# Loading two token groups of a hybrid layer in both layouts, instead of transposing them on TensorE

## The chip, the cores and the metric

The kernel runs on one core of one Trainium2 chip. Its time is the device time of one execution in microseconds (us). A core has a matrix engine (TensorE, PE in the profile, with PEld for its weight loads), a vector engine (VectorE, DVE), a scalar engine (ScalarE, ACT), GpSimd (POOL) and SyncE (SP), whose queue issues most of the DMA transfers here. Each engine works through its own list of instructions in order and waits on semaphores for the others. On-chip data lies in SBUF, and matmul results land in PSUM; 128 partitions each.

## The reference

One layer of a hybrid network over 1280 tokens: 256 context tokens (`ctx`) and 1024 latent tokens (`x`), 1024 features each. Cut to what matters for the change, its first step is

```
h   = rms_norm(tokens, g)                     # per token: x * rsqrt(mean(x*x) + 1e-6) * g
h   = h * (1 + scale) + shift                 # per feature; scale, shift from c (latents) or c_ctx (context)
u   = h @ w_in                                # one combined input projection, 1024 features in
...                                           # short convs, gated delta rule, retention, gates,
...                                           # output projection, residual, SwiGLU, residual, final norm
```

The factor of the norm belongs to a token; gain, scale and shift belong to a feature. All of it is float32 in the reference.

## The kernel before

**Stages.** The program runs in five parts, by the trace: the stage "h" (modulated tokens, first columns of the projection; to about 111 us), the rest of the projection with short convolutions (to about 300), chunks of the gated delta rule and retention (to about 580), and then the output projection and the SwiGLU part up to 1476 us.

**The stage "h".** Matmuls contract over the partition axis, so the tokens are needed with features on partitions: `hhi` and `hlo` hold the modulated tokens as eight tiles (index `k`, 128 features each) by 1280 tokens. A float32 value is split in two: `hhi` is the value rounded to the short format `fp32r`, `hlo` what is left. The product with a weight `whi + wlo` is then three matmuls (`tm_half`, L366 to L373: `whi·hhi` on L371, `wlo·hhi` on L372, `whi·hlo` on L373), 24 of them for a token tile of 128 tokens and a group `g` of output columns (272 columns for g=0, 256 for g=1).

**Token groups.** Tiles of 128 tokens are handled in four groups, `XGROUPS = [[2, 3], [4, 5], [6, 7, 8, 9], [0, 1]]` (tiles 0 and 1 are the context). In the text they are called group 0 to 3. For each group:

- `normalize` (L319): ACT squares each token tile and sums it (L325), DVE takes the reciprocal root (`rsqrt_mean`, last instruction L139), and DVE multiplies each loaded tile, tokens on partitions, by its factors in place (L328).
- `turned` (L330): PE transposes 128x128 blocks through a matmul with `ident` into a PSUM bank `xtr` (L334); one bank holds one `k` of all the group's tokens.
- `modulate` (L307): ACT writes `hhi` from that bank with scale and shift as per-partition operands (L311), DVE computes the same value in full float32 as `hf` (L313, two buffers), and `hlo = hf - hhi` is computed by DVE for even `k` and by GpSimd for odd `k` (L314).
- PE runs the 24 matmuls for each tile, first all tiles of the group for g=0, then for g=1; three PSUM banks `tm` take the results, ACT copies them out (L384 and L402), and they are stored.

The modulated tokens of group 2 are made while PE works on group 1, those of group 3 while PE works on group 2.

**What sets the order.** The program text goes through a scheduler that simulates the engines and fixes each engine's list. An edit can therefore move rows that it doesn't touch. The loads of this stage are chained one behind the other on SyncE's queue by `in_order` (L235); the token tiles have seven buffers.

**Behind the stage.** `ada_rest` loads more modulation weights (`adaw2`, L495), accumulates them on DVE (L497, L499, into `acc`) and sums over partitions on PE (L504, into `gr`). The convolution part of the projection starts with L611. Its buffers take the room of the stage's own, so its loads on SyncE's queue wait until that is free.

Of the kernel before, what the change touches and what calls it, by code (L numbers as in the profile page):

```python
# [8 lines left out]
F32 = mybir.dt.float32  # L9
# [8 lines left out]
P = 128  # L18
# [20 lines left out]
def build(nc, tc, ap, dbg=None, stop=None, marks=None):  # L39
# [19 lines left out]
    def close(p):  # L59
        p_close.pop(id(p)).close()  # L60
# [130 lines left out]
    try:  # L191
# [115 lines left out]
        def modulate(src, k, j, sl):  # L307

            n = sl.stop - sl.start
            a, b = amix[:, j, k:k + 1], bmix[:, j, k:k + 1]  # L310
            hh = S.activation(hhi[:, k, sl], src, AF.Identity, bias=b, scale=a)  # L311
            hf = P0.tile([P, 512], F32, tag="hf", name="hf", bufs=2)
            V.tensor_scalar(hf[:, :n], src, a, b, ALU.mult, ALU.add)  # L313
            (G if k % 2 else V).tensor_tensor(hlo[:, k, sl], hf[:, :n], hhi[:, k, sl].bitcast(F32), ALU.subtract)  # L314
            return hh.ins

        XGROUPS = [[2, 3], [4, 5], [6, 7, 8, 9], [0, 1]]

        def normalize(gi, hold=None):  # L319
            grp = XGROUPS[gi]  # L320
            ms = P0.tile([P, len(grp)], F32, tag="ms%d" % gi, name="ms")
            with tc.issue_after(hold) if hold is not None else nullcontext():
                for i, t in enumerate(grp):
                    junk = P0.tile([P, D], F32, tag="junk", name="junk", bufs=1)
                    S.activation(junk, xts[t], AF.Square, accum_out=ms[:, i:i + 1])  # L325
                rstd = rsqrt_mean(P0, ms, len(grp), "rx%d" % gi, D)
            for i, t in enumerate(grp):
                V.tensor_scalar(xts[t], xts[t], rstd[:, i:i + 1], None, ALU.mult)  # L328

# [7 lines left out]
        def modulated(gi):  # L337
            grp = XGROUPS[gi]
            for k in range(KT):
                end = modulate(turned(gi, k, bank_b), k, 1 if grp[0] == 0 else 0, slice(grp[0] * P, (grp[-1] + 1) * P))  # L340
            return end

        def split(raw, hi, lo, e):
# [100 lines left out]
            begin(3)  # L444
        ada_end = coefficients(1)
        close(PA)
        W2 = pool("w2", bufs=2)
        xa = W2.tile([P, TT, 16], F32, tag="xa", name="xa", bufs=1)
        raw_weights(1, 0, W2)
# [3 lines left out]
        for n in ("alog", "dtb"):  # L453
            small[n] = C.tile([P, 8], F32, tag=n, name=n)
            in_order(small[n], ap[n].partition_broadcast(P))
        for t in (6, 7, 8, 9, 0, 1):
            load_x(t)
        hold = None
        for k in range(4, KT):
            hold = modulate(xnT[:, k, :], k, 0, slice(2 * P, 4 * P))  # L460
        normalize(1, hold)
        for gi, grp in enumerate(XGROUPS):
            for g in range(2):
                if gi == 0 and g == 1:
                    for kh in range(2):
                        wr[1, kh] = tm_weights(1, kh, W2)
                for t in grp:
                    if (g, t) in first:
                        o = first[g, t]
                    else:  # L470
                        o = tm_bank(g)
                        tm_half(o, wr[g, 0], 0, t)
                    tm_half(o, wr[g, 1], 1, t)
                    tm_store(g, t, o, fin_copy, S, W2)
                if g == 0 and gi + 1 < len(XGROUPS):
                    hold = modulated(gi + 1)
            if gi + 2 < len(XGROUPS):
                normalize(gi + 2, hold)
        close(P0)
        checkpoint("h")  # L480

# [1129 lines left out]
def prepare(inputs):  # L1611
# [2 lines left out]
    a = {}  # L1614
    a["x"] = f(inputs["x"])[0]
    a["ctx"] = f(inputs["ctx"])[0]
    a["cc"] = f(np.stack([np.asarray(inputs["c"])[0], np.asarray(inputs["c_ctx"])], -1).reshape(KT, P, 2).transpose(1, 0, 2))
    ada_w = np.asarray(inputs["ada_w"])[0]
    a["ada1"] = f(ada_w[:, :2 * D].reshape(KT, P, 2, 2, 512).transpose(3, 0, 1, 2, 4))
# [35 lines left out]
```

## Time and profile before

| what | value |
|---|---|
| median of 3 runs | 1481.49 us (1479.01 to 1481.59) |
| profiled execution | 1477.96 us, span 1476.2 us |
| mean granted TensorE clock | 0.983 |
| PE busy | 1397.2 us, 95% |
| DVE busy | 964.6 us, 65% |
| ACT busy | 614.0 us |
| POOL busy | 590.3 us |

A row of a timeline gives the start in us, the duration in us, the engine, the source line, the operation, output and inputs by their names in the program, the tile's shape, and after "x" how many of them follow each other; in square brackets stands how long the engine had been idle before, and what released it. A row of windows gives a stretch of time, and for each engine the time busy in it with the number of instructions. Source lines (L...) are lines of the kernel before unless said otherwise.

### The profile page before, as it was taken

The numbers are of one execution on the slowest core, as the hardware profiler recorded it, in microseconds if no ns is written. First come the engines' busy times: TensorE is split into PE (matmuls) and PEld (weight loads), VectorE is DVE, ScalarE is ACT, GpSimd is POOL, SyncE is SP. The second block draws the span as 40 slices with busy tenths as digits, with TensorE's granted clock in tenths as the row PEclk, the third lists the DMA queues.
The fourth block names the chain that finished last, engine by engine and source line by source line (L and its number), as shares of the span: only waits on it lengthen the run. The fifth ranks groups of instructions, "written<-read, shape, count | busy, mean of one in ns | idle before, by whom it ended". The sixth has DMA issues, their size and how long they took to land.

```text
span 1476.2 us, 24111 instructions
## 1 busy us (share of the span) xinstructions
PE 1397.2 (95%) x8919; PEld 1199.2 (81%) x8919; DVE 964.6 (65%) x1856; ACT 614.0 (42%) x1326; POOL 590.3 (40%) x501
## 2 busy tenths in 40 slices
PE   7999999986789999899799899999999999999997
PEld 2898888975689999898688688877888888788885
DVE  6566789289792435689676877556555564657477
ACT  5643564587333111245443623233333332444445
POOL 0120010243202344234144688898555552335321
PEclk9999999998899999999899999999999999999999
DMA  9536686688888625996532265674222242776863
GB/s 337 197 105 205 189 249 200 219 264 277 282 216 277 238 76 178 416 341 209 184 125 104 97 238 210 242 264 162 105 97 105 107 151 79 260 260 194 288 216 114
DMA packets 170421, 298.14 MB, mean 202 GB/s; under 512 B 43496, under 2 KB 93880, under 8 KB 165952
## 3 DMA queue, kind: packets, MB, share of 16 engines
q1 hardware_dynamic: 118752, 253.17, 50.2%
q10 hardware_dynamic: 49072, 35.83, 7.8%
q0 software_dynamic: 2480, 7.60, 1.4%
q8 instruction: 70, 1.15, 0.3%
q14 instruction: 47, 0.39, 0.1%
HBM read 206.60 MB, written 89.96 MB: 201 GB/s over the span
## 4 chain that ended last, share of the span: by engine, by line
PE 55%; POOL 6%; DMA 5%; DVE 4%; issue 2%; ACT 2%; SPq 1%; ACTq 0%; POOLq 0%; DVEq 0%
PE ffn L1344 7%; PE ffn L1342 6%; PE ffn L1343 6%; PE fo L1470 4%; PE fo L1469 4%; PE fo L1468 4%; PE tm L371 3%; PE tm L373 3%; PE tm L372 3%; PE op L1203 2%; PE op L1201 2%; PE op L1202 2%; DMA wd<-tw 2%; POOL ws L1315 1%; DMA pk<-sd 1%
## 5 line engine op out<-in xcount | busy, mean ns | idle before, releaser
L371 PE MATMUL tm<-whi,hhi 128*128 128x256 f32 (+1 forms) x704 | 199.5, 287 | 7.7 <-ACT vt L859 3.4
L372 PE MATMUL tm<-wlo,hhi 128*128 128x256 f32 (+1 forms) x704 | 199.3, 285 | 2.4 <-issue 2.0
L373 PE MATMUL tm<-whi,hlo 128*128 128x256 f32 (+1 forms) x704 | 197.7, 285 | 0.0
L371 PEld LDWEIGHTS tm<-whi,hhi 128*128 128x128 f32 x704 | 132.8, 190 | 11.8 <-ACT vt L859 3.6
L1342 PE MATMUL ffn<-t,whi 128*128 128x512 f32 x352 | 136.9, 390 | 1.3 <-ACT whi L344 1.3
L1344 PE MATMUL ffn<-t,wlo 128*128 128x512 f32 x352 | 137.0, 390 | 1.0 <-DVE wlo L345 1.0
L1343 PE MATMUL ffn<-t,whi 128*128 128x512 f32 x352 | 137.0, 389 | 0.0
L372 PEld LDWEIGHTS tm<-wlo,hhi 128*128 128x128 f32 x704 | 133.7, 190 | 2.1 <-issue 0.9
L373 PEld LDWEIGHTS tm<-whi,hlo 128*128 128x128 f32 x704 | 132.8, 190 | 2.6 <-issue 1.8
L344 ACT ACTIVATE whi<-wraw 128x512 fp32r<-128x512 f32 (+2 forms) x98 | 75.1, 771 | 141.4 <-PE ffn L1343 80.5
L344 ACT ACTIVATE whi<-ws 128x512 fp32r<-128x512 f32 x88 | 55.6, 632 | 171.5 <-PE ffn L1343 123.4
L345 DVE TENSOR_TENSOR wlo<-ws,whi 128x512 fp32r<-128x512 f32 x88 | 93.9, 1068 | 47.0 <-ACT whi L344 46.8
L1469 PE MATMUL fo<-wlo,ahi 128*128 128x512 f32 x308 | 120.2, 390 | 2.1 <-DVE wlo L345 2.1
L1468 PE MATMUL fo<-whi,ahi 128*128 128x512 f32 x308 | 119.3, 390 | 0.7 <-ACT ahi L344 0.7
L1470 PE MATMUL fo<-whi,alo 128*128 128x512 f32 x308 | 119.0, 390 | 0.0
L345 DVE TENSOR_TENSOR wlo<-wraw,whi 128x512 fp32r<-128x512 f32 (+2 forms) x92 | 99.4, 1082 | 24.6 <-ACT whi L344 24.6
L1342 PE MATMUL ffn<-b,whi 128*128 128x512 f32 x264 | 103.8, 393 | 4.4 <-ACT whi L344 4.4
L1344 PE MATMUL ffn<-b,wlo 128*128 128x512 f32 x264 | 103.6, 393 | 0.8 <-DVE wlo L345 0.8
L1343 PE MATMUL ffn<-b,whi 128*128 128x512 f32 x264 | 103.4, 392 | 0.0
L612 PE MATMUL b<-hlo,whi 128*128 128x512 f32 (+1 forms) x256 | 94.4, 369 | 0.0
L613 PE MATMUL b<-hhi,wlo 128*128 128x512 f32 (+1 forms) x256 | 94.3, 368 | 0.0
L611 PE MATMUL b<-hhi,whi 128*128 128x512 f32 (+1 forms) x256 | 94.3, 368 | 0.0
(446 smaller groups left out, 3448.1 us busy)
## 6 DMA issues: line engine op xcount, KB each, us to landing
adaw<-ada SPq DMA_DIRECT2D x48, 512.0 KB, 4.4
pk<-sd SPq DMA_DIRECT2D x16, 1536.0 KB, 10.0
wraw<-wfi SPq DMA_DIRECT2D x44, 512.0 KB, 3.7
ar<-ad SPq DMA_DIRECT2D x33, 512.0 KB, 4.7
w<-wfo SPq DMA_DIRECT2D x22, 512.0 KB, 5.7
wd<-tw SPq DMA_DIRECT2D x11, 1024.0 KB, 4.8
ad<-act SPq DMA_DIRECT2D x20, 512.0 KB, 3.0
raw<-wd SPq DMA_DIRECT2D x20, 512.0 KB, 4.9
```

Of the source, the lines that this page charges most:

```text
L344: S.activation(hi, raw, AF.Copy)
L345: e.tensor_tensor(lo, raw, hi.bitcast(F32), ALU.subtract)
L371: T.matmul(o, hhi[:, k, tsl], whi[:, k % 4, :], start=(k == 0), stop=False)
L372: T.matmul(o, hhi[:, k, tsl], wlo[:, k % 4, :], start=False, stop=False)
L373: T.matmul(o, hlo[:, k, tsl], whi[:, k % 4, :], start=False, stop=(k == KT - 1))
L612: T.matmul(o, whi[:, k, :], hl, start=False, stop=False)
L1342: T.matmul(o, whi[:, k, :], xhi(xn, slice(0, 4), k), start=(first and k == 0), stop=False, **kw)
L1343: T.matmul(o, whi[:, k, :], xlo(xn, slice(0, 4), k), start=False, stop=False, **kw)
L1344: T.matmul(o, wlo[:, k, :], xhi(xn, slice(0, 4), k), start=False, stop=(k == 3), **kw)
L1468: T.matmul(po[g][i], ahi[:, ts], whi, start=(j == 0 and not kw), stop=False, **kw)
L1469: T.matmul(po[g][i], ahi[:, ts], wlo, start=False, stop=False, **kw)
L1470: T.matmul(po[g][i], alo[:, ts], whi, start=False, stop=(j == FH - 1), **kw)
```

## The change

For groups 2 and 3 the tokens are also loaded with features on partitions, from a second copy of the tokens in device memory that is stored that way (`xT`): eight tiles of 128x512 for group 2 and eight of 128x256 for group 3, in eight buffers of one size. The tiles with tokens on partitions are still loaded, since the sums of squares are taken from them. The in-place scaling of these tiles (L328) and the transposes (L334) of the two groups are gone. In their place the factors of a group are turned into a row that is the same on all partitions: for each token tile `ident` is multiplied by the factors (DVE, tile `diag`, two buffers), a matmul of `ones` with that diagonal puts the factors on every partition (PE, bank `rrow`), DVE copies the bank to SBUF, and each `xT` tile is multiplied by it in place (DVE). `modulate` then reads `xT` in SBUF instead of a PSUM bank. Lines of the changed kernel below the first added block stand 9 lines further down, then 18, 23, 24, 28 and, behind the stage, 29.

```
+        def load_xT(gi):
+            grp = XGROUPS[gi]
+            for k in range(KT):
+                xt = PX[0].tile([P, 512], F32, tag="xT", name="xT", bufs=8)
+                xTs[gi, k] = xt[:, :len(grp) * P]
+                in_order(xTs[gi, k], ap["xT"][k, :, grp[0] * P:(grp[-1] + 1) * P])
...
         def normalize(gi, hold=None):
...
+            if gi >= 2:
+                pr = bank_b("rrow")
+                for i in range(len(grp)):
+                    dg = PX[0].tile([P, P], F32, tag="diag", name="diag", bufs=2)
+                    V.tensor_scalar(dg, ident, rstd[:, i:i + 1], None, ALU.mult)
+                    T.matmul(pr[:, i * P:(i + 1) * P], ones, dg, start=True, stop=True)
+                rrow[gi] = PX[0].tile([P, 512], F32, tag="rrow", name="rrow", bufs=1)
+                V.tensor_copy(rrow[gi][:, :len(grp) * P], pr[:, :len(grp) * P])
+                return
             for i, t in enumerate(grp):
                 V.tensor_scalar(xts[t], xts[t], rstd[:, i:i + 1], None, ALU.mult)
...
         def modulated(gi):
             grp = XGROUPS[gi]
             for k in range(KT):
-                end = modulate(turned(gi, k, bank_b), k, 1 if grp[0] == 0 else 0, slice(grp[0] * P, (grp[-1] + 1) * P))
+                if gi >= 2:
+                    src = xTs[gi, k]
+                    V.tensor_tensor(src, src, rrow[gi][:, :len(grp) * P], ALU.mult)
+                else:
+                    src = turned(gi, k, bank_b)
+                end = modulate(src, k, 1 if grp[0] == 0 else 0, slice(grp[0] * P, (grp[-1] + 1) * P))
...
         close(PA)
+        PX.append(pool("px", side="right"))
...
-        for t in (6, 7, 8, 9, 0, 1):
+        for t in (6, 7, 8, 9):
             load_x(t)
+        load_xT(2)
+        for t in (0, 1):
+            load_x(t)
+        load_xT(3)
...
+        close(PX[0])
         close(P0)
...
+    a["xT"] = f(np.concatenate([a["ctx"], a["x"]], 0).T.reshape(KT, P, NTOK))
```

On the vector engine the work for group 2 changes its order. Names here: `rx2y` are the factors of group 2's tokens, `rrow` is the row of factors (bank and copy). Before, from the scaling of group 2's tiles on:

```order
L328 TENSOR_SCALAR xt<-xt,rx2y 128x1024 x4
L313 TENSOR_SCALAR hf<-xtr,amix,bmix 128x512 x2
L314 TENSOR_TENSOR hlo<-hf,hhi 128x512
L313 TENSOR_SCALAR hf<-xtr,amix,bmix 128x512 x2
```

and in the changed kernel at the same place:

```order
L340 TENSOR_SCALAR diag<-ident,rx2y 128x128 x4
L343 COPY rrow<-rrow 128x512
L360 TENSOR_TENSOR xT<-xT,rrow 128x512 x8
L313 TENSOR_SCALAR hf<-xT,amix,bmix 128x512 x2
L314 TENSOR_TENSOR hlo<-hf,hhi 128x512
```

All eight multiplications stand ahead of the first `hf` and the first `hlo`, where before the first `hf` followed the scaling directly.

On TensorE, the end of group 1's work and the start of group 2's (the first rows with 272 columns), before:

```order
L373 MATMUL tm<-whi,hlo 128x256
L334 MATMUL xtr<-ident,xt 128x128 x12
L371 MATMUL tm<-whi,hhi 128x272
L372 MATMUL tm<-wlo,hhi 128x272
L371 MATMUL tm<-whi,hhi 128x272
L372 MATMUL tm<-wlo,hhi 128x272
L371 MATMUL tm<-whi,hhi 128x272
L372 MATMUL tm<-wlo,hhi 128x272
L334 MATMUL xtr<-ident,xt 128x128 x8
L373 MATMUL tm<-whi,hlo 128x272
```

and in the changed kernel (its L394, L395 and L396 are L371, L372 and L373 of before):

```order
L396 MATMUL tm<-whi,hlo 128x256
L341 MATMUL rrow<-diag,ones 128x128 x4
L394 MATMUL tm<-whi,hhi 128x272
L395 MATMUL tm<-wlo,hhi 128x272
L394 MATMUL tm<-whi,hhi 128x272
L395 MATMUL tm<-wlo,hhi 128x272
L394 MATMUL tm<-whi,hhi 128x272
L395 MATMUL tm<-wlo,hhi 128x272
L396 MATMUL tm<-whi,hlo 128x272
```

The transposes are gone and four matmuls with `ones` stand where the first twelve were; the first matmul with `hlo` still stands behind three pairs with `hhi`, as before.

On SyncE's queue the eight loads of group 2's `xT` come between the last latent tiles and the first context tile, and those of group 3 behind the second context tile:

```order
L238 DMA xt<-x 128x1024 x4
L238 DMA xT<-xT 128x512 x8
L238 DMA xt<-ctx 128x1024
L377 DMA wraw<-wt 128x1024 x2
L238 DMA xt<-ctx 128x1024
L238 DMA xT<-xT 128x256 x8
L524 DMA adaw_1240<-ada 128x1024
```

Before, the same rows stood there without the two of `xT`; the first of the `adaw` loads (L495 before, L524 now) comes behind them.

More of the change, by code (lines that the diff above doesn't have):

```diff
@@ L315, in modulate @@
             return hh.ins
+        xTs, rrow, PX = {}, {}, []
+        def load_xT(gi):
[4 more added lines that the diff above has]
+                in_order(xTs[gi, k], ap["xT"][k, :, grp[0] * P:(grp[-1] + 1) * P])
         XGROUPS = [[2, 3], [4, 5], [6, 7, 8, 9], [0, 1]]
```

## The prediction

> **What bounds the kernel now.** I read first how busy the engines are in each stretch of the program, cut where TensorE changes its work: end of group 1, group 2 with g=0, group 2 with g=1, group 3, the convolution part, the chunks. Columns: each engine's busy time with instructions, the granted TensorE clock, the DMA share and GB/s.
>
> ```profile
> core 0: us, PE busy (x) PEld busy (x) DVE busy (x) ACT busy (x) POOL busy (x), PEclk, DMA share, GB/s
> 60.00:68.37 8.37, 7.08 (x58) 6.87 (x57) 2.87 (x10) 6.04 (x15) 0.74 (x1) 1.00 0.35 110
> 68.37:83.35 14.98, 13.82 (x107) 12.52 (x105) 11.45 (x20) 9.26 (x17) 5.90 (x4) 1.00 0.13 45
> 83.35:99.63 16.28, 16.28 (x137) 16.28 (x137) 7.64 (x17) 7.85 (x19) 3.16 (x4) 1.00 0.31 100
> 99.63:111.37 11.74, 11.74 (x98) 11.74 (x97) 9.14 (x14) 4.19 (x10) 2.39 (x1) 1.00 0.64 207
> 100.00:300.00 200.00, 200.00 (x1229) 175.52 (x1228) 142.79 (x244) 99.70 (x275) 23.33 (x20) 1.00 0.68 215
> 300.00:480.00 180.00, 147.48 (x2005) 135.41 (x2004) 134.68 (x275) 92.81 (x233) 45.81 (x48) 0.94 0.87 262
> ```
>
> TensorE is busy all the time from 83 to 300 us, so there what delays it delays the end, and work taken off it in group 2's second half and in group 3 is time saved. The one place where the changed work meets something else is 68.37 to 83.35: TensorE lacks 1.16 of 14.98 us, and VectorE is at 11.45 us, the next bound. So I read that stretch row by row, first on TensorE.
>
> ```profile
> 68.37 1.94 PE L334 MATMUL xtr<-ident,xt 128*128 128x128 f32 x12
> 70.97 0.39 PE L371 MATMUL tm<-whi,hhi 128*128 128x272 f32 x1 [0.65 <-ACT hhi L311]
> 71.82 1.39 PE L334 MATMUL xtr<-ident,xt 128*128 128x128 f32 x8
> 73.16 0.39 PE L373 MATMUL tm<-whi,hlo 128*128 128x272 f32 x1
> 75.53 1.03 PE L334 MATMUL xtr<-ident,xt 128*128 128x128 f32 x8
> 78.64 0.60 PE L334 MATMUL xtr<-ident,xt 128*128 128x128 f32 x4
> 83.35 0.39 PE L371 MATMUL tm<-whi,hhi 128*128 128x272 f32 x1 [0.30 <-ACT xa L384]
> 99.63 0.29 PE L371 MATMUL tm<-whi,hhi 128*128 128x272 f32 x1
> 111.37 0.28 PE L611 MATMUL b<-hhi,whi 128*128 128x256 f32 x1
> ```
>
> The 32 transposes of group 2 come in four lots among the matmuls of its first three tiles; the fourth tile starts at 83.35. Then VectorE, GpSimd and ScalarE in the same place:
>
> ```profile
> 66.77 0.16 DVE L139 SCALAR_TENSOR_TENSOR rx2y<-rx2u,rx2y 128x4 f32<-128x4 f32 x1
> 66.97 2.74 DVE L328 TENSOR_SCALAR xt<-xt,rx2y 128x1024 f32<-128x1024 f32 x4
> 70.95 1.56 DVE L313 TENSOR_SCALAR hf<-xtr,amix,bmix 128x512 f32<-128x512 f32 x2 [1.24 <-ACT hhi L311]
> 72.42 0.68 DVE L314 TENSOR_TENSOR hlo<-hf,hhi 128x512 fp32r<-128x512 f32 x1
> 78.85 1.17 DVE L314 TENSOR_TENSOR hlo<-hf,hhi 128x512 fp32r<-128x512 f32 x1
> 72.58 1.66 POOL L314 TENSOR_TENSOR hlo<-hf,hhi 128x512 fp32r<-128x512 f32 x1 [10.72 <-DVE hf L313]
> 78.17 1.29 POOL L314 TENSOR_TENSOR hlo<-hf,hhi 128x512 fp32r<-128x512 f32 x1 [1.35 <-DVE hf L313]
> 70.13 2.12 ACT L311 ACTIVATE hhi<-xtr,bmix,amix 128x512 fp32r<-128x512 f32 x3 [1.18 <-PE xtr L334]
> ```
>
> The factors are there at 66.93, and the first `hlo` at 73.10; the first matmul that reads it (L373) starts at 73.16. That handover sets the pace, and it is what I follow through the change.
>
> **The change part by part. The row of factors.** Four diagonals of 128x128 on VectorE stand for 2.74 us of scaling. No row has this shape; the nearest are
>
> ```profile
> 29.54 0.73 DVE L313 TENSOR_SCALAR hf<-xnT,amix,bmix 128x256 f32<-128x256 f32 x2
> 31.84 1.02 DVE L313 TENSOR_SCALAR hf<-xnT,amix,bmix 128x256 f32<-128x256 f32 x2
> 30.75 1.64 POOL L314 TENSOR_TENSOR hlo<-hf,hhi 128x256 fp32r<-128x256 f32 x1 [30.31 <-ACT hhi L311]
> 99.37 0.48 DVE L497 TENSOR_SCALAR acc<-adaw,csl 128x512 f32<-128x512 f32 x1
> 276.29 1.95 PE L705 MATMUL kk<-kc 128*128 128x128 f32 x16
> L932 DVE COPY S<-up x2: 691/692/692, 485.2 to 486.1; 128x512 f32<-128x512 f32 x2
> 830.13 1.88 DVE L345 TENSOR_TENSOR wlo<-wraw,whi 128x512 fp32r<-128x512 f32 x3
> ```
>
> Half of 0.73 is 0.37 at 256 columns, so 0.2 to 0.37 at 128; I take 0.3. Diagonals 0 and 1 are done by 67.6, and TensorE is free from group 1 at 68.37. A float32 matmul of 128x128 shows as two passes, 1.95/16 = 0.12 each, so 0.24. With two `diag` buffers, diagonals 2 and 3 wait for the first two matmuls; the four matmuls end near 69.95. The copy from PSUM costs 0.69 (the only row of that size): the row stands at 70.65, where before the scaled tiles stood at 69.71.
>
> **The multiplications.** Eight of 128x512 with both inputs in SBUF. L345's row gives one such as 0.68 (also the lone `hlo`) and then 1.88 - 0.68 = 1.20 for two, 0.60 each. The eight take 0.68 + 7·0.60 = 4.9 us, to 75.5, and by the order on VectorE all stand ahead of the first `hf`. Then two `hf`, now from SBUF instead of PSUM: 0.48 and 0.44 (L497's row, 0.48, against 1.56/2 = 0.78 before), to 76.45, and `hlo` 0.68, to 77.1. ScalarE is no limit: the first `hhi` can start when the first multiplication ends, 71.3, and ends 2.12/3 = 0.7 later, 72.0; TensorE's first L371 moves from 70.97 to 72.1, does three pairs, and waits for the first `hlo`: from 73 to 77.1. Before, transposes filled part of that time; they are gone, so the gap is bare.
>
> **What this makes of group 2.** From 77.1, 66 of the 72 matmuls of three tiles remain, at 11.74/98 = 0.12 (last stage in the windows): 7.9 us, to 85.0, and with the wait of 0.30 before it the fourth tile starts at 85.3 instead of 83.35: +2.0. That holds if the later `hlo` keep up. They keep up only if GpSimd's and VectorE's shares run side by side. The rows say that they don't: the `hlo` at 78.85 took 1.17, and ended at 80.02, which is 79.46 (GpSimd's end) + 0.56, where the lone one took 0.68; the pair of `hf` from SBUF at 31.84 took 1.02 instead of 0.73 with GpSimd running until 32.39. Before, `hf` read PSUM and shows no such wait; now all of VectorE's work there reads SBUF. With strict turns (GpSimd 1.1 of its own) the `hlo` of k = 0 to 7 come at 77.1, 78.3, 79.4, 81.6, 82.2, 84.7, 85.4 and 87.35, the fourth tile starts at 88.1: +4.7. The Trainium skill (SBUF — State Buffer, "Who interferes with whom") states that a VectorE instruction with two SBUF inputs or in a two-port mode and a GpSimd instruction that reads SBUF exclude each other for a whole instruction; by that rule the upper of the two sums holds, and the trace's 1.17 against 0.68 agrees.
>
> **Group 3.** Its 16 transposes lie in the full stretch from 83.35 to 99.63:
>
> ```profile
> 86.83 0.49 PE L334 MATMUL xtr<-ident,xt 128*128 128x128 f32 x3
> 91.17 0.38 PE L334 MATMUL xtr<-ident,xt 128*128 128x128 f32 x2
> ```
>
> Three take 0.49 with a last drain of 0.29, so 0.10 each at the least, and 0.15 by the lot at 68.37 ((1.94-0.29)/11): 1.6 to 2.4 us, I take 1.7. Its two matmuls for the row cost 2·0.24 = 0.5, so -1.2. VectorE has the room for the rest: 7.64 of 16.28 us are busy, and two scalings go while eight multiplications of half the size come (about 8·0.35 = 2.8 us). The stage as a whole: +0.8 without exclusion, +3.5 with; nearest to the rows is the second, and I take **+3.0**.
>
> **Behind the stage.** The sums that the convolution part starts with:
>
> ```profile
> 111.30 0.65 DVE L499 SCALAR_TENSOR_TENSOR acc<-adaw,csl,acc 128x512 f32<-128x512 f32 x1
> 113.13 1.02 PE L504 MATMUL gr<-acc,ones 128*1 128x512 f32 x2
> ```
>
> `acc` is done at 111.95, 0.58 after TensorE's stage ends at 111.37. The matmul on it (L504) stood some 15 matmuls behind the first L611; in the new order it stands ahead of it. If the chain moves with the stage, TensorE waits about 0.6 us: **+0.5**, between 0 (the chain is not moved) and +1.5. The added 3 MB of loads fall on a DMA share of 0.13 to 0.35, and the weights behind them are first used after 104 us: 0, and what would uncover them is the second rival. The order also differs between 280 and 480 us, where TensorE lacks 180 - 147.48 = 32.5 us; I know no sign for that: 0, between -3 and +3.
>
> **Sum:** 3.0 + 0.5 = +3.5. The profiled execution took 1477.96 us, 3.5 below the median; I add the difference to the median: 1481.49 + 3.5 = **1485.0**.
>
> **The rivals.** (a) No change that can be measured (0.2% is about 3 us): the engines overlap after all, +0.8 in the stage, and the later order gives or takes two: 1479.5 to 1484, middle 1482. For it: GpSimd's idle of 1.35 between its `hlo` shows slack. Against it: the gap before the first L373 does not depend on the overlap. (b) SyncE's queue.
>
> ```profile
> 70.87 14.67 SPq L495 DMA_DIRECT2D adaw<-ada  x2
> 59.71 0.33 SPq L238 DMA_DIRECT2D xt<-ctx  x1
> ```
>
> The eight loads of group 3's `xT` each wait for a buffer of group 2, freed as late as 87 by the last `hf`, and the `adaw` loads (before: waited until 85.2) stand behind them. If the first of these then lands 3 us later than the stage moves, the whole chain to L504 does, and TensorE stands at L504: +3 more, 1488. Against it: these loads waited for the stage's memory anyway, and the last four are paced by `acc`. (c) The other side: the saving comes through. If the scheduler's list doesn't hold `hlo` back (the first by 73 us, as when the multiplications run between the `hf`), 5.1 us of transposes of group 2 (1.94 + 1.39 + 1.03 + 0.60 = 4.96 by the rows, with the pauses at their ends) and 1.2 us of group 3 are gone, less 1 us for the later row of factors: about -5, 1476. The point from which it decides is a first `hlo` before about 74 us. Against it: the list has all eight multiplications first.
>
> **How the numbers follow.** My forecast gets 0.45, with a range of its own from +1 to +7: 0.30 of it slower by over 0.2%, 0.15 within. Rival (a) 0.25: 0.22 within, 0.03 faster. Rival (b) 0.15, slower. Rival (c) 0.15: 0.10 faster, 0.05 within, where part of the saving is eaten. Together: faster 0.13, same 0.42, slower 0.45. The range: 1478.5 leaves out most of (c), 1491 some of (b) and the top of the later order's luck, together about 0.18. The likeliest case alone runs from 1482.5 to 1488.5.
>
> **What the profile will show.** Right if eight multiplications of about 0.6 us stand on VectorE from about 70.7 to 75.5; if TensorE then idles about 4 us before its first matmul with `hlo`, released by VectorE; if `hlo` rows on either engine stretch past their lone durations; if the fourth tile of group 2 starts 2 to 5 us later than 83.35, the convolution part 1 to 4 later than 111.37, and 111 to 300 keeps its length within 1 us. Wrong if the first `hlo` comes by 74 us, if the multiplications take 0.4 us or less, or if most of the difference arises after 280 us, where I set it to 0.

## The result

| | median | runs | ratio to before |
|---|---|---|---|
| before | 1479.24 us | 9, 1477.88 to 1481.59 | |
| changed | 1486.66 us | 9, 1481.74 to 1488.86 | 1.0041, 95% interval 1.0028 to 1.0054 |

The change makes the kernel slower by 0.41%, 6.1 us (0.0041 · 1479.24). The two medians lie 7.4 us apart, which is inside the interval of the ratio (4.1 to 8.0 us); the sums below go by the 6.1. The forecast was +3.5 us and slower, with a range from 1478.5 to 1491. The profiled execution of the changed kernel took 1486.66 us (span 1484.8, granted clock 0.974 against 0.983).

### The profile after

First the place where all was expected to happen, the start of group 2. Windows of the changed kernel, with the columns of the table shown for the kernel before:

```profile
69.00:73.92 4.92, 2.41 (x20) 2.03 (x18) 3.00 (x8) 1.25 (x3) 0.00 (x0) 0.92 0.14 46
73.92:78.80 4.88, 1.72 (x6) 1.40 (x6) 4.84 (x10) 4.88 (x8) 0.51 (x1) 0.50 0.01 3
78.80:83.28 4.48, 4.48 (x20) 4.48 (x21) 4.38 (x6) 2.50 (x6) 2.56 (x2) 0.50 0.45 127
83.28:90.00 6.72, 6.46 (x47) 5.88 (x47) 6.08 (x17) 0.84 (x4) 2.94 (x2) 0.99 0.25 73
```

TensorE (first busy time) works 4.1 of 9.8 us between 69 and 78.8. VectorE (third) works 3.00 of 4.92 us in the first window, where it waits for TensorE's row of factors (1.30 and 0.58 us), and 4.84 of 4.88 us in the second. The granted clock is at half (0.50) from 73.2 to 83.4. Before, TensorE worked 13.82 of the 14.98 us from 68.37 to 83.35, and the clock was 1.00. TensorE's rows of the changed kernel:

```profile
70.85 0.71 PE L341 MATMUL rrow<-diag,ones 128*128 128x128 f32 x4 [0.16 <-DVE diag L340]
73.92 0.59 PE L394 MATMUL tm<-whi,hhi 128*128 128x272 f32 x1 [2.35 <-ACT hhi L311]
75.22 0.43 PE L395 MATMUL tm<-wlo,hhi 128*128 128x272 f32 x1
78.80 0.60 PE L396 MATMUL tm<-whi,hlo 128*128 128x272 f32 x1 [3.16 <-DVE hlo L314]
79.20 0.43 PE L394 MATMUL tm<-whi,hhi 128*128 128x272 f32 x1
79.42 0.43 PE L395 MATMUL tm<-wlo,hhi 128*128 128x272 f32 x1
90.72 0.29 PE L394 MATMUL tm<-whi,hhi 128*128 128x272 f32 x1
105.14 0.28 PE L394 MATMUL tm<-whi,hhi 128*128 128x272 f32 x1
120.93 0.39 PE L640 MATMUL b<-hhi,whi 128*128 128x512 f32 x1
```

The two waits are the ones forecast, first for `hhi`, then for the first `hlo`. At 79.20 and 79.42 matmuls of 272 columns follow each other in 0.22 us, where 0.12 is usual. The row at 90.72 is the start of the fourth tile, the one at 105.14 group 3. The last row is the point by which I read all runs below: **S**, the start of the first matmul with 512 columns in the convolution part. It is 120.93 here, and before:

```profile
115.36 0.40 PE L611 MATMUL b<-hhi,whi 128*128 128x512 f32 x1
```

So the first stage ends 5.57 us later. VectorE's rows of the changed kernel, from the last instruction of group 2's factors:

```profile
68.52 0.16 DVE L139 SCALAR_TENSOR_TENSOR rx2y<-rx2u,rx2y 128x4 f32<-128x4 f32 x1
71.60 0.69 DVE L343 COPY rrow<-rrow 128x512 f32<-128x512 f32 x1 [0.58 <-PE rrow L341]
72.32 4.91 DVE L360 TENSOR_TENSOR xT<-xT,rrow 128x512 f32<-128x512 f32 x8
77.14 1.00 DVE L313 TENSOR_SCALAR hf<-xT,amix,bmix 128x512 f32<-128x512 f32 x2
78.06 0.69 DVE L314 TENSOR_TENSOR hlo<-hf,hhi 128x512 fp32r<-128x512 f32 x1
78.78 1.39 DVE L313 TENSOR_SCALAR hf<-xT,amix,bmix 128x512 f32<-128x512 f32 x1
81.80 1.27 DVE L128 TENSOR_SCALAR rx3x<-ms 128x2 f32<-128x2 f32 x1
```

and GpSimd's in the same place:

```profile
78.29 1.60 POOL L314 TENSOR_TENSOR hlo<-hf,hhi 128x512 fp32r<-128x512 f32 x1 [14.68 <-DVE hf L313]
81.57 1.47 POOL L314 TENSOR_TENSOR hlo<-hf,hhi 128x512 fp32r<-128x512 f32 x1 [1.68 <-DVE hf L313]
87.29 1.39 POOL L314 TENSOR_TENSOR hlo<-hf,hhi 128x512 fp32r<-128x512 f32 x1 [1.35 <-DVE hf L313]
```

The factors end at 68.68, 1.75 later than before (66.93). I split the stage there: what lies ahead of the factors, and **A**, from the factors to S, 115.36 - 66.93 = 48.43 before and 120.93 - 68.68 = 52.25 now. The eight multiplications take 4.91 us, the first `hlo` ends at 78.75, and the last (GpSimd, 87.29 + 1.39) at 88.68. The row at 81.80 shows the turns best: an instruction on 128x2 elements took 1.27 us, while GpSimd ran from 81.57 to 83.04. At 78.78 an `hf` took 1.39 where a lone one takes 0.55, and ended 0.28 behind GpSimd's end at 79.89.

What lies ahead of the factors, 1.75 us, is there in this execution before any changed work starts. TensorE's first matmul with 272 columns is as late already, and it starts before the first `xT` load is issued (41.18). Here it is before and in the changed kernel:

```profile
38.42 0.40 PE L371 MATMUL tm<-whi,hhi 128*128 128x272 f32 x1
40.15 0.39 PE L394 MATMUL tm<-whi,hhi 128*128 128x272 f32 x1
```

Of the 1.73 us, 0.36 were there at 35 us (a row at 34.92 before is at 35.28), and the rest is the clock, which was at half for 3.4 us from 35.6, in work that the change doesn't touch; the kernel before had no such drop in its profile. From this matmul to the factors it is 28.51 us before and 28.53 now.

The `xT` loads do show on ScalarE. Its rows before (columns: start, duration, engine; ACTq rows are its DMA issues):

```profile
47.99 0.38 ACTq L387 DMA_DIRECT2D rd<-res  x1
48.18 0.20 ACT L384 ACTIVATE xa<-tm 128x16 f32<-128x16 f32 x1
```

and in the changed kernel:

```profile
49.91 0.20 ACT L407 ACTIVATE xa<-tm 128x16 f32<-128x16 f32 x1
51.69 0.99 ACTq L410 DMA_DIRECT2D rd<-res  x2
52.97 0.39 ACT L425 ACTIVATE res<-tm 128x256 f32<-128x256 f32 x1 [2.85 <-PE tm L396]
```

Before, the first store of results was issued at 47.99, right behind the copy of its results (which ended at 47.96). Now that copy ends at 49.69, and the store is issued 2.0 us later, at 51.69, while SyncE issues the burst of group 2's `xT`:

```profile
41.18 8.74 SPq L238 DMA_DIRECT2D xT<-xT  x8
```

Here this costs nothing: the copy at 52.97 waits for TensorE, 2.85 us as in the kernel before. In the runs below where the clock didn't drop early, the factors come 0.7 to 1.6 us later than before, counted from the first matmul with 272 columns. The prediction had these loads on a DMA share of 0.13 to 0.35. Those of group 2, 2 of the 3 MB, were issued from 41.18 to 49.92, at a share of 0.92, and before the change that stretch was at 0.95.

### The profile page after: what moved, and what is told of

It reads as the page before. It is cut to its first block, busy times and chain, and to the rows that moved or that the text cites. A ratio compares the mean times of both kernels' runs of the same rounds, so it can differ in the third digit from the quotient of the medians.

```text
span 1484.8 us, 24101 instructions
## 1 busy us (share of the span) xinstructions
PE 1403.6 (95%) x8883; PEld 1204.6 (81%) x8883; DVE 975.1 (66%) x1874; ACT 614.9 (41%) x1326; POOL 592.0 (40%) x501
## 4 chain that ended last, share of the span: by engine, by line
PE 56%; DMA 6%; POOL 4%; issue 3%; DVE 3%; ACT 1%; SPq 1%; ACTq 0%; POOLq 0%; DVEq 0%
PE ffn L1373 8%; PE ffn L1372 7%; PE ffn L1371 7%; PE fo L1497 4%; PE fo L1498 4%; PE fo L1499 4%; PE tm L396 3%; PE tm L395 3%; PE tm L394 3%; PE op L1230 2%; PE op L1231 2%; PE op L1232 2%; DMA wd<-tw 1%; PE up L958 1%; PE Tr L951 1%
## 5 line engine op out<-in xcount | busy, mean ns | idle before, releaser
L394 PE MATMUL tm<-whi,hhi 128*128 128x256 f32 (+1 forms) x704 | 201.5, 291 | 7.1 <-ACT hhi L311 2.8
L396 PE MATMUL tm<-whi,hlo 128*128 128x256 f32 (+1 forms) x704 | 200.9, 289 | 3.4 <-DVE hlo L314 3.2
L395 PE MATMUL tm<-wlo,hhi 128*128 128x256 f32 (+1 forms) x704 | 202.8, 290 | 0.5 <-DVE wlo L368 0.5
L394 PEld LDWEIGHTS tm<-whi,hhi 128*128 128x128 f32 x704 | 135.8, 195 | 10.2 <-ACT hhi L311 3.2
L396 PEld LDWEIGHTS tm<-whi,hlo 128*128 128x128 f32 x704 | 136.0, 194 | 4.5 <-DVE hlo L314 3.7
L395 PEld LDWEIGHTS tm<-wlo,hhi 128*128 128x128 f32 x704 | 136.9, 195 | 2.4 <-issue 0.9
```

The source lines that it names most:

```text
L394: T.matmul(o, hhi[:, k, tsl], whi[:, k % 4, :], start=(k == 0), stop=False)
L395: T.matmul(o, hhi[:, k, tsl], wlo[:, k % 4, :], start=False, stop=False)
L396: T.matmul(o, hlo[:, k, tsl], whi[:, k % 4, :], start=False, stop=(k == KT - 1))
```

## The experiments

All are timed against the kernel before, in the same way as the change. Each edit also makes the scheduler order the work behind the stage anew, which matters for reading them; I call that order the list behind the stage. S, A and the column "S to Y" come from one profiled execution of each. **Y** is the first transpose of the output projection; between S and Y stands work that no edit touches. The cuts of code show the lines that matter; the rest of each edit passes names along.

| kernel | S | A | S to Y | ratio, 95% interval | us |
|---|---|---|---|---|---|
| before | 115.36 | 48.43 | 596.1 | | |
| changed | 120.93 | 52.25 | 602.7 | 1.0041 (1.0028 to 1.0054) | +6.1 |
| turns | 118.92 | 50.75 | 599.7 | 1.0027 (1.0014 to 1.0041) | +4.0 |
| dve | 119.95 | 51.15 | 603.8 | 1.0039 (1.0025 to 1.0054) | +5.8 |
| warm | 120.54 | 51.53 | 598.7 | 1.0042 (1.0028 to 1.0057) | +6.2 |
| loads | 116.02 | 48.44 | 596.2 | 0.9997 (0.9989 to 1.0006) | -0.4 |
| g3 | 115.16 | 47.19 | 604.9 | 1.0041 (1.0025 to 1.0057) | +6.1 |
| g2 | 122.08 | 53.82 | 606.6 | 1.0083 (1.0065 to 1.0100) | +12.3 |
| early | 117.45 | | 599.0 | 1.0027 (1.0013 to 1.0040) | +4.0 |
| both | 117.07 | | 596.7 | 1.0028 (1.0013 to 1.0043) | +4.1 |
| stores | 119.68 | 52.25 | 600.0 | 1.0041 (1.0027 to 1.0055) | +6.1 |
| neutral | 116.91 | 48.48 | 600.2 | 1.0036 (1.0022 to 1.0051) | +5.3 |
| fusedsp | 111.87 | | 599.9 | 1.0007 (0.9993 to 1.0022) | +1.0 |
| fused4 | 110.62 | | 602.2 | 1.0000 (0.9983 to 1.0017) | 0.0 |

"us" is (ratio - 1) · 1479.2. A is left out where the factors are made at another time.

### turns: multiplication, hf and hlo alternate

```
                     src = xTs[gi, k]
-                    V.tensor_tensor(src, src, rrow[gi][:, :len(grp) * P], ALU.mult)
+                    with tc.issue_after(hv) if hv is not None else nullcontext():   # hv: hf of the k before
+                        V.tensor_tensor(src, src, rrow[gi][:, :len(grp) * P], ALU.mult)
```

> Edit: each multiplication is queued on VectorE behind the hf of the tile before it, so that multiplication, hf and hlo alternate; nothing else is edited, and the rows behind the first stage stand nearly as in the kernel before (a dozen places differ, against some 75 for the changed kernel). Measured are two stretches: A from the end of group 2's factors to the first 512-column matmul of the convolution part (48.4 us before, 52.25 changed), B from there to the end (1360.8 before, 1363.9 changed). Theory 'list and turns' (my prediction: all eight multiplications ahead of the first hlo, and VectorE and GpSimd exclude each other): the first hlo comes about 4 us sooner (about 6 us behind the factors instead of 10.1), but VectorE's work is the same and the last hlo gains only about 1 us, so A is 50 to 51.5. Rival 'list alone' (only the late first hlo costs): A falls by 4, to about 48. Theory 'later order' (part of the +6 comes from the rows behind the first stage): B is that of before, 1361 within 1.5, and the median at least 2.5 us under that of the changed kernel; rival 'no later order': B as changed.

VectorE's rows in this run:

```profile
71.80 0.69 DVE L362 TENSOR_TENSOR xT<-xT,rrow 128x512 f32<-128x512 f32 x1
72.53 0.55 DVE L313 TENSOR_SCALAR hf<-xT,amix,bmix 128x512 f32<-128x512 f32 x1
72.99 0.68 DVE L362 TENSOR_TENSOR xT<-xT,rrow 128x512 f32<-128x512 f32 x1
73.59 0.68 DVE L314 TENSOR_TENSOR hlo<-hf,hhi 128x512 fp32r<-128x512 f32 x1
75.37 1.38 DVE L313 TENSOR_SCALAR hf<-xT,amix,bmix 128x512 f32<-128x512 f32 x1
```

The first `hlo` ends at 74.27, 6.1 us behind the factors (68.17) instead of 10.07, as expected; the last ends at 87.2, 19.1 behind them instead of 20.0, and A is 50.75, within the 50 to 51.5 of "list and turns". "List alone" (A about 48) is out: it is VectorE's whole work for the group that sets the pace, and the 1.38 us of an `hf` show the turns again. "Later order" gets nothing from this run. It asked for B (from S to the end) of 1361; with a list nearly like the old one, B is 1364.9 in the profile, no better than the changed kernel's 1363.9, and by the ratios the run is 2.1 us faster than the changed kernel, as much as S gained (2.0).

### dve: no GpSimd in groups 2 and 3

```
-            (G if k % 2 else V).tensor_tensor(hlo[:, k, sl], hf[:, :n], hhi[:, k, sl].bitcast(F32), ALU.subtract)
+            (G if k % 2 and not (sl.start == 0 or sl.start == 6 * P) else V).tensor_tensor(hlo[:, k, sl], hf[:, :n], hhi[:, k, sl].bitcast(F32), ALU.subtract)
```

> Edit: in groups 2 and 3 every hlo is on VectorE, none on GpSimd; behind the first stage TensorE's and VectorE's lists are those of the changed kernel row by row. Theory 'list and turns': without GpSimd each tile takes 0.46 + 0.69 us of VectorE, the last hlo of group 2 comes 8 * 1.15 = 9.2 us behind the eighth multiplication instead of 11.5, A falls by 1.5 to 2.3, to about 50.3, and no hf or hlo row is longer than its lone duration. Rival 'no exclusion': VectorE has four hlo more, the last hlo comes 2.8 us later than with GpSimd at its side, A rises to 53 or more. B is that of the changed kernel by both, 1363 to 1364, if its order costs what that one profile shows.

```profile
77.29 1.00 DVE L313 TENSOR_SCALAR hf<-xT,amix,bmix 128x512 f32<-128x512 f32 x2
78.20 1.28 DVE L314 TENSOR_TENSOR hlo<-hf,hhi 128x512 fp32r<-128x512 f32 x2
79.41 1.00 DVE L313 TENSOR_SCALAR hf<-xT,amix,bmix 128x512 f32<-128x512 f32 x2
80.32 1.28 DVE L314 TENSOR_TENSOR hlo<-hf,hhi 128x512 fp32r<-128x512 f32 x2
```

VectorE's rows here: four more `hlo` for VectorE, and yet the last `hlo` comes at 86.2, 17.4 us behind the factors (68.80) instead of 20.0, and no row is stretched. That is the test of the turns: taking GpSimd's help away makes the last `hlo` come 2.6 us sooner. A fell by 1.1, less than the 1.5 to 2.3 expected, since TensorE was still at half clock (76.6 to 83.4 in this run) and had a backlog when the last `hlo` came.

### warm: matmuls in the gap

```
+                if gi == 2:
+                    wm = bank_c("warm")
+                    with tc.issue_after(mm.ins):                        # mm: last matmul of the row
+                        for _ in range(48):
+                            T.matmul(wm[:, 0:WIDE], hhi[:, 0, 2 * P:3 * P], wr[0, 0][0][:, 0, :], start=True, stop=True)
```

> Edit: 48 matmuls of 128x272 into a bank that nobody reads stand behind the four matmuls of group 2's row of factors, 48 * 0.123 = 5.9 us of work in the time in which TensorE waited (2.35 + 3.16 us); output unchanged. The changed kernel's profile shows half the TensorE clock from 73.2 to 83.4 and matmuls at 0.226 instead of 0.123 there. Theory 'clock' (the gap drops the clock, and the slow matmuls cost): no half clock in this stretch, TensorE has no backlog when the last hlo comes, the fourth tile starts 0.7 us behind it instead of 2.0, A falls by about 1.3, to 51. Theory 'list and turns' alone: the hlo set the pace whatever the clock, A stays at 52.25 within 0.4.

TensorE's rows:

```profile
71.65 6.26 PE L346 MATMUL warm<-whi,hhi 128*128 128x272 f32 x48
79.14 0.40 PE L401 MATMUL tm<-whi,hlo 128*128 128x272 f32 x1 [0.47 <-DVE hlo L314]
83.44 0.39 PE L401 MATMUL tm<-whi,hlo 128*128 128x272 f32 x1 [0.64 <-POOL hlo L314]
90.23 0.39 PE L399 MATMUL tm<-whi,hhi 128*128 128x272 f32 x1 [0.30 <-ACT xa L412]
```

The clock stays at 1.00 in this stretch, and TensorE now waits for `hlo` again and again (0.47, 0.64). The fourth tile starts 21.2 us behind the factors (69.01), not 22.0, and A is 51.53: 0.7 less. So the half clock cost 0.7 us, half of what "clock" gave it; the pace of the `hlo` is the larger part. The ratio didn't move with it (+6.2 us).

### loads: xT is loaded, nobody reads it

```
-            if gi >= 2:                       # in normalize and in modulated
+            if gi >= 4:
```

> Edit: xT is loaded as in the changed kernel but nobody reads it, and groups 2 and 3 are scaled and transposed as before; the lists of TensorE, VectorE and ScalarE behind the first stage are those of the kernel before, row by row. Theory 'list and turns': the 3 MB of loads are hidden, A is 48.4 within 0.5, the median within 1.5 us of before. Rival 'SyncE's queue or DMA': the added loads delay the loads behind them or the first stage, A or the start of group 2 is 1 us or more later, the median 2 us or more over before.

A is 48.44 and the ratio 0.9997, so the loads as such cost nothing that the median shows. But ScalarE's wait is there:

```profile
51.94 0.38 ACT L425 ACTIVATE res<-tm 128x256 f32<-128x256 f32 x1 [3.63 <-DMA xT<-xT]
```

ScalarE stood 3.63 us and the profile names the `xT` transfer; 2.85 of them it stood before too, waiting for TensorE. Group 2's factors end at 67.58 instead of 66.93, and S is 0.66 later. TensorE's list behind the stage is the kernel before's here, row by row.

### g3 and g2: one group each

```
-            if gi >= 2:                       # in normalize and in modulated; load_xT of the other group is left out
+            if gi >= 3:                       # g3;  g2: if gi == 2:
```

> Edit: the change for group 3 alone; group 2 is scaled and transposed as before, its xT is not loaded. S is the start of the first 512-column matmul of the convolution part (115.4 us before, 120.9 changed). Theory 'list and turns' (all of the loss is in group 2): 1.7 us of transposes go, 0.5 us of matmuls come, VectorE has room, S falls by 1 to 1.5 against before, to about 114.2, and the loads of group 3, behind 59 us, meet no store: ScalarE's first store of the stage is issued where it was before (48 us). Rival 'the row costs wherever it stands': S is not under 115.4. The list behind the stage differs in many places; the median is 1478.0 if that is worth nothing.

> Edit: the change for group 2 alone; group 3 is scaled and transposed as before, its xT is not loaded. Theory 'list and turns': all of the loss and none of group 3's gain: the stretch from group 2's factors to the first 512-column matmul of the convolution part is 52.25 + 1.4 = 53.6 us (48.4 before), the ratio to before 1.004 to 1.0055, not under that of the changed kernel. Rival 'loads': ScalarE's first store of the stage (issued at 48.0 before, at 50.9 to 52.4 in every kernel that loads group 2's xT so far) is at 50 or later here too, and at 48 in the run with group 3 alone; by it 0.6 to 2 us of the loss stand before group 2's factors.

Group 3 alone: the factors of group 2 are 1.0 us late in this execution (from its first microseconds on), and S is at 115.16, so A is 47.19: a gain of 1.24 us, as the prediction had it. ScalarE's first store is issued at 49.04, against 51.55 with group 2 alone. Group 2 alone: A is 53.82, 5.4 us of loss, no gain. The sum of the two, 5.4 - 1.2 = 4.2, is close to the 3.8 of the changed kernel.

The times tell something else as well. With group 3 alone the stage is not longer at all, and the kernel is 6.1 us slower. Two rows of this run, S and the first transpose of the output projection:

```profile
115.16 0.39 PE L639 MATMUL b<-hhi,whi 128*128 128x512 f32 x1
720.03 1.04 PE L1215 MATMUL yT<-ident,yt 128*128 128x128 f32 x8
```

and that transpose before:

```profile
711.48 1.04 PE L1187 MATMUL yT<-ident,yt 128*128 128x128 f32 x8
```

Between the two points the run lost 8.7 us (604.87 against 596.12), in work that no edit touches. That is one execution, at 1487.58 us the slowest of its six, and by the ratio the kernel lost 6.1 in all. With group 2 alone the ratio gives a loss of 12.3 where S lost 6.7.

### neutral: the kernel before, four stores on SyncE

```
-                    tm_store(g, t, o, fin_copy, S, W2)
+                    tm_store(g, t, o, fin_copy, SY if gi == 0 else S, W2)
```

> Edit to the kernel before: group 0's four stores are issued by SyncE; no xT, no other change. The first stage keeps its order but for these stores; behind it TensorE's list differs in 37 places and VectorE's in 48, as a result of the scheduler. Theory 'later order' (the run with group 3 alone lost nothing in the stage, yet 6 us in sum, between 360 and 700 us): S stays 115.4 within 0.7 and the ratio can lie off 1 by 0.1 to 0.4%, either way, with the difference arising behind 280 us. Rival 'order is worth nothing': the ratio is 1 within 0.1%.

```profile
116.91 0.40 PE L611 MATMUL b<-hhi,whi 128*128 128x512 f32 x1
717.14 1.04 PE L1187 MATMUL yT<-ident,yt 128*128 128x128 f32 x8
```

A is 48.48, so nothing changed in the stage (S is 1.55 later, with the clock at half for 3.4 us at 35.1 again). The ratio is 1.0036: four stores on another queue, in a stage that they don't hold up, cost 5.3 us. "Order is worth nothing" is out. Where the 5.3 us lie this profile doesn't show. From S to the output projection it lost 4.1 us (600.23 against 596.12), but it won 3.8 back from there to the end, and it is the fastest of the twelve executions. That the list behind the stage costs them is inferred: it is what differs behind the stage, and "loads", another program with the old list, costs nothing.

### stores: the changed kernel with the same four stores on SyncE

The edit is that of "neutral".

> Edit to the changed kernel: the four stores of group 0's results are issued by SyncE instead of ScalarE; nothing else. Theory 'queue' (with the burst of eight xT loads under way, ScalarE stands at its first store until 50.9 to 52.4 instead of 48.0, and what follows on it, evictions, hhi and squares, is late): ScalarE does not stand there, group 2's factors are done 0.6 to 2 us sooner than in the changed kernels without this edit (68.2 to 69.0), at about 67 to 67.5 if TensorE's clock does not drop at 35 us, and S (first 512-column convolution matmul; 118.9 to 120.9 so far) is lower by the same; the stretch from the factors to it stays at 52.25 within 0.5. Rival 'list and turns alone': the factors are no sooner.

ScalarE no longer stands there, and the factors end at 67.43 (no drop of the clock at 35 us in this run), which is within the 67 to 67.5 expected; A is 52.25, to the digit that of the changed kernel. Of the kernels that load group 2's `xT`, keep the stores on ScalarE and had no early drop of the clock either, the factors end at 67.58 (loads), 68.17 (turns), 68.26 (g2) and 69.01 (warm). These executions don't all start alike, so I count from the first matmul with 272 columns: 28.49 us to the factors here, 28.51 in the kernel before, and 29.23, 29.61, 29.59 and 30.09 in those four. The queue's part is 0.7 to 1.6 us, 1.1 on average, in an execution without the early drop of the clock. The ratio stayed at 1.0041, with another list behind the stage again.

### early and both: the factors sooner

```
-                normalize(gi + 2, hold)
+                normalize(gi + 2, hold[3 if gi == 0 else -1])       # hold: all hhi of the group, not the last
```

> Edit: the squares of group 2's tokens are queued on ScalarE behind the fourth hhi of group 1 instead of behind the last, so that the row of factors is made about 4 us sooner, while TensorE still works on group 1; all eight multiplications still stand ahead of the first hlo. Theory 'list and turns': the first hlo comes about 4 us sooner against the end of group 1's matmuls, the last too, S falls by about 4 against the changed kernel, to 117 or less; TensorE waits under 2 us before its first matmul with hlo, and has no or a shorter half clock there. Rival 'ScalarE is the limit': the squares push group 1's hhi back by as much (four of 1.25 us), and S stays within 1 us of 120.9.

> Edit: the early squares and the alternating multiplications together. Theory 'list and turns': the first hlo is there when TensorE ends group 1, the following ones come every 1.9 us on average while a third of the matmuls needs 24 * 0.123 / 3 of them... in sum VectorE and GpSimd need 8 * (0.6 + 0.46) + 4 * 0.68 + 4 * 1.1 = 15.6 us for group 2 against 72 * 0.123 = 8.9 us of matmuls of three tiles, so VectorE still sets the pace, from about 64.5 on: the last hlo at about 83, the fourth tile at 83.5 to 84.5, S 112.5 to 114.5 and the median 1476 to 1478, faster than both kernels. Rival 'only the first hlo counts': S about 111. Rival 'loads': ScalarE's store behind the burst of xT loads holds group 1's hhi and the early squares, S 115 or more and the median not under that of before.

The factors end at 64.51 and 65.01, 4 us sooner, and S is 117.45 and 117.07: 3.5 and 3.9 us sooner than in the changed kernel, and with the alternating multiplications hardly better than without. Both stay short of what I expected (S to 114.5 for the second). Part of it is the clock, at half near 35 us in both. The rest stands in the order: with two `diag` buffers the third and fourth matmul of the row had been put behind some twenty matmuls of group 1, and the copy of the row waited 2.65 us for them. VectorE's work remained the bound, and the ratios are 1.0027 and 1.0028.

### fusedsp and fused4: less work on VectorE

```
-                    V.tensor_tensor(src, src, rrow[gi][:, :len(grp) * P], ALU.mult)
-                end = modulate(src, k, 1 if grp[0] == 0 else 0, slice(grp[0] * P, (grp[-1] + 1) * P))
+                    with tc.issue_after(hl[-2]) if len(hl) > 1 else nullcontext():
+                        V.scalar_tensor_tensor(src, src, amix[:, j, k:k + 1], rrow[gi][:, :len(grp) * P], ALU.mult, ALU.mult)
+                    S.activation(hhi[:, k, sl], src, AF.Identity, bias=bmix[:, j, k:k + 1])
+                    hl.append(V.scalar_tensor_tensor(hlo[:, k, sl], src, bmix[:, j, k:k + 1], hhi[:, k, sl].bitcast(F32), ALU.add, ALU.subtract).ins)
```

Both have the early squares; the first has the four stores on SyncE, the second four `diag` buffers.

> Edits to the changed kernel: squares early, group 0's stores on SyncE, and for groups 2 and 3 one instruction makes xT times scale times row, ScalarE adds the shift into hhi, and one VectorE instruction adds the shift and subtracts hhi into hlo; hf and GpSimd's part are gone, the multiplication for k+1 stands ahead of the hlo of k. VectorE's work for group 2 falls from 8 * (0.6 + 0.46) + 4 * 0.68 to about 8 * (0.65 + 0.68) = 10.6 us with nobody to take turns with. Theory 'list and turns': the first hlo is there when TensorE comes, the last about 12 us behind the row, near 79; the fourth tile starts by 81 (83.35 before), S is 111 to 113 against 115.4 before: 2.5 to 4.5 us faster, if the rows behind the stage cost nothing; the ratio 0.997 to 0.999, or up to 1.003 if they cost what they do in the run with group 3 alone. Rival 'something else holds the stage': S over 114.5.

> Edits: as in the kernel with the fused VectorE instructions, but group 0's stores stay on ScalarE and diag has four buffers, which gives another list behind the stage. Theory 'later order' (the first stage and the list behind it are two separate terms): S is 112 to 114 (111.9 with the stores on SyncE, and 0.6 to 2 more for ScalarE standing behind the xT loads), and the ratio is that gain of 1.5 to 3.5 us plus a draw of the list, 0 to 6 us: 0.998 to 1.003. Rival 'the gain in the stage is always given back': the ratio is 1.000 to 1.001 again with a list that differs from the last one's.

VectorE's rows of the first:

```profile
67.47 0.69 DVE L343 COPY rrow<-rrow 128x512 f32<-128x512 f32 x1 [2.66 <-PE rrow L341]
68.19 1.42 DVE L363 SCALAR_TENSOR_TENSOR xT<-xT,amix,rrow 128x512 f32<-128x512 f32 x2
69.74 0.75 DVE L365 SCALAR_TENSOR_TENSOR hlo<-xT,bmix,hhi 128x512 fp32r<-128x512 f32 x1
70.41 0.75 DVE L363 SCALAR_TENSOR_TENSOR xT<-xT,amix,rrow 128x512 f32<-128x512 f32 x1
```

Two instructions of 0.66 us each for a tile, none of them stretched. The last `hlo` ends at 79.3, the fourth tile starts at 81.16 (83.35 before), and S is 111.87, 3.5 us sooner than before; with four `diag` buffers the copy comes at 65.57, and S is 110.62, 4.7 us sooner, better than expected though its stores stayed on ScalarE. So the stage can be shorter with the loads than it was with the transposes, once VectorE isn't the bound. How much of this is due to the loads is open: both kernels also have the early squares, and no run has those together with the transposes. Neither beats the kernel before: 1.0007 and 1.0000. The gain is lost behind the stage: in fused4's profile the first output transpose stands 1.3 us later than before, not 4.7 sooner. "Given back always" would fit the two, but "neutral" lost without having gained, and "loads", with the old list, lost nothing; no run here has the shorter stage with the old list, so whether the gain could be kept is open.

## Why the prediction was right, and where not

**Right, by its own steps.** The row of factors was put at 3.72 us behind the factors and took 3.61. The multiplications: 4.9, and 4.91. The first `hlo`: 10.17 behind the factors, measured 10.07. The taking of turns: last `hlo` 20.4 behind the factors, measured 20.0; "dve" shows that it is turns and not load, since less help was faster. The Trainium skill (SBUF — State Buffer, "Who interferes with whom"), by which the upper sum was to hold, agrees with that: 1.27 us for an instruction on 128x2 elements beside GpSimd's. Group 3: -1.2 forecast, -1.24 in the run with it alone. The prediction took +3.0 for the stage out of 0.8 to 3.5; A grew by 3.8, a little over the upper end.

**Its signs.** The eight multiplications of 0.6 us came, and so did TensorE's wait for the first `hlo`, 3.16 us behind another of 2.35. From S to the first matmul of the chunks it is 160.7 us against 160.9 before, so the stretch up to 280 us kept its length, and of the 8.6 us between the two profiles' ends 5.3 are there at that matmul. The stretched rows are not VectorE's `hlo` (0.68 and 0.69), but its `hf` and its instructions on two columns. Two places were set too early: the fourth tile starts 7.4 us later than before (5.6 counted from the factors), not 2 to 5, and the convolution part's first matmuls, now those on `acc`, start at 117.03 instead of 111.37, 5.7 later, not 1 to 4.

**The half clock was missing.** The upper sum, +3.5, held nothing for the clock; the gap that I saw coming takes it to half, and the slow matmuls cost 0.7 us by "warm". I had followed the gap only as waiting. The Trainium skill (TensorE: Matmul & The Clock Gate, "HAM oscillation — how this bites in real kernels") warns of idle gaps over 3.4 us; here the clock fell at 73.2, 1.6 us into the gap of 2.35, and the two gaps ahead of it lasted 0.16 and 1.30 us, so no gap of that length was needed.

**"The added 3 MB fall on a low DMA share: 0" was wrong.** Group 2's 2 MB were issued where the share was 0.95 before, and ScalarE's stores, on a queue of its own, had to wait behind them: 0.66 us on S in "loads", 0.7 to 1.6 us ahead of the factors by "stores". In the changed kernel's own profile the early drop of the clock hides it. My rival on SyncE's queue looked for the harm at the `adaw` loads behind `xT`, which were not late: the last sum on `acc` ended at 108.8, well ahead of L504's place, so the +0.5 "behind the stage" was 0 too. The Trainium skill (DMA: Bandwidth & Descriptors, "Issuing engines are not separate DMA queues") states that transfers issued by different engines share the same DMA engines; the 3.63 us of ScalarE in "loads", 2.85 of them there before, show that here.

**"The later order: 0, between -3 and +3" held here, but was too narrow for such lists, and it has a sign.** Subtracting S's delay from the time leaves +0.5 us for the changed kernel and -1.1 for "loads" with the old list. For the other ten lists it leaves 0.4 (turns), 1.0 (warm), 1.8 (stores), 1.9 (early), 2.4 (both), 3.8 (neutral), 4.5 and 4.7 (the fused ones), 5.6 (g2) and 6.3 (g3). Each rests on S of one profile, which alone moves by 1 to 1.7 us. So none of the eleven lists was clearly better than the old one, and five were clearly worse. The column "S to Y" points the same way: the two pairs of kernels with one list agree (596.1 and 596.2 with the old one; 602.7 and 603.8 for the changed kernel and "dve"), and the other lists lie at 596.7 to 606.6. By it the changed kernel lost 6.6 us up to Y and won 3.5 back from Y to the end, 3.0 behind S in all. Why a list costs what it does, no run shows.

In sum, of the 6.1 us (4.1 to 8.0 by the interval) 3.8 are group 2's late `hlo`, less group 3's gain and with 0.7 of it the clock; "turns", "dve", "warm", "g2" and "g3" show that. The other 2.3 us these runs can't split: ScalarE behind the `xT` burst is worth 0.7 to 1.6 us in an execution without the early drop of the clock and nothing in the one profiled, and the list behind the stage 0.5 to 3. The mechanism forecast was right; the sizes that were off are the clock, the loads and the sums on `acc`, and the sum came out at 3.5 instead of 6.1. That it stayed in the range is in part luck: with a list that costs 6.3, as in "g3", and the same stage, the time would have been about 1491 (1479.2 + 5.6 + 6.3), the end of the range.

## What to carry to other kernels

Replacing TensorE's work by another layout moves it to the engine that has to apply the factors; add up that engine's whole work for the group, with the turns it takes with its neighbour, before counting the transposes as saved. Then fuse that work: two `scalar_tensor_tensor` in place of the multiplication, `hf` and `hlo`, together with the early squares, made the stage 3.5 to 4.7 us shorter than it had been. In a program whose order comes from a scheduler, run an edit that changes nothing else first: here such an edit was worth 0.36%, nearly as much as the change's 0.41%.

## What was not expected of the hardware

A store on ScalarE's queue was issued 2.0 us behind its copy in the changed kernel, and 3.0 in "loads" (copy until 47.87, issue at 50.88), while SyncE had eight loads of 256 KB under way; before it was 0.03. ScalarE's next copy came 0.8 us later for it in "loads" (3.63 us of waiting instead of 2.85). An instruction of 2 columns on VectorE took 1.27 us beside a GpSimd instruction, eight times the 0.16 of its like. TensorE's clock was granted at half in pieces of 3.4, 6.8 or 10.2 us up to S, at about 35 us in five of the fourteen kernels' profiles and not in the others, in work that is the same in all of them.
